# Roots for four latent heads at once, decay matrices by two wide products, and a first stage with its squares on VectorE and its rotary tables later

## The chip, the core and the metric

The kernel runs on one core of one Trainium2 chip. The core has five engines that run side by side, each through a list of its own: TensorE (PE in the profile; its weight loads are shown as PEld), VectorE (DVE), ScalarE (ACT), GpSimd (POOL) and SyncE (SP), which here issues the transfers between the chip's memory and the core's. The metric is device time in microseconds for one execution; smaller is better. The kernel before has a median of 1480.11 us over three runs (1479.24 to 1482.22).

## The reference

The program computes a four-part decoder trunk of two layers on x with 1024 tokens and 1024 channels, all in 32-bit floats. Cut to what the change touches:

```
def rmsnorm(x, g):
    xf = x.astype(jnp.float32)
    y = xf * lax.rsqrt(jnp.mean(xf * xf, axis=-1, keepdims=True) + EPS)
    return (y * g.astype(jnp.float32)).astype(x.dtype)
...
def even_layer(h, layer_idx, positions, w_in, ...):
    z = h @ w_in                       # h is rmsnorm(x)
    a_in, a_gate, q, k, v, b_gate = _split(z, EVEN_WIDTHS)
    ...
    q = partial_rope(rmsnorm(q, q_norm), positions, B_ROT, ROPE_THETA)
    k = partial_rope(rmsnorm(k, k_norm), positions, B_ROT, ROPE_THETA)
...
def odd_layer(h, positions, w_in, ...):
    q = (rmsnorm(cq, q_a_norm) @ w_uq).reshape(B, T, H_C, DQK_C)
    kv = (rmsnorm(ckv, kv_a_norm) @ w_ukv).reshape(B, T, H_C, D_NOPE + DV_C)
    ...
    q = rmsnorm(q, q_norm)             # 4 heads of 192, one root for each token and head
    k = rmsnorm(k, k_norm)
...
def gated_delta_rule(q, k, v, g, beta):
    gc = jnp.cumsum(g, axis=-1)
    gamma = jnp.exp(jnp.where(incl, gc[..., :, None] - gc[..., None, :], -jnp.inf))
```

Layer 0 holds a pooling mixer and differential attention, layer 1 latent attention (4 heads) and a gated DeltaNet (4 heads). Each layer ends in an output projection and a gated per-layer embedding.

## The kernel before

**Tiling.** Tokens are cut into blocks of 128 (eight of them, in two halves of 512), channels into chunks of 128 (eight). A large product is done with both operands split into a high and a low part in the F32R type, as three products of up to 512 columns (`mm3`, L142 to L144): high by high, high by low, low by high. The split is one ScalarE copy (L134, or L137 with a scale) and one VectorE subtract (L135, or L138). A product of plain F32 operands appears in the profile as two TensorE instructions. The eight accumulator banks of 512 columns have tags: acc (2), s (2), x (2), tr (1) and o (1).

**What sets the order.** Every engine runs its own list in order. The lists are laid out when the program is built, by a scheduler that goes by the order of the program and by estimated times, so that work later in the program can stand ahead of earlier work that is not ready by estimate: the profile shows a memset of L414 at 0.81 us, long before the loop of L356 begins.

**The first stage (0 to about 69 us).** The first loop (L356) goes over the eight chunks of x's first half. `load_x` (L322) loads a chunk, splits it (L137, L138) and squares it on ScalarE (L329, L332); from the second chunk on GpSimd adds the square to a running sum (L333). `wload` loads and splits the weights of the pool branch (L134, L135), and twelve products follow. After the second chunk the program has `rope_tables` (L193 to L230), which builds the cosine and sine of layer 0 from the positions: 56 VectorE instructions on tiles of at most 128x64, two Sin on ScalarE, four GpSimd writes. Their constants (the inverse frequencies) are loaded by a transfer of their own ahead of them, and another transfer after the loop (L369) loads the rest of the constants.

The second loop does the same for x's second half, with nine products a chunk. After its third chunk `finish_x(0)` turns the first half's sums into roots: eight small TensorE instructions (L182), ten small VectorE instructions (L121, L111 to L116, iterations of a root in integer and float steps), two copies, a VectorE product with the unit matrix (L187), a product with a matrix of ones (two TensorE instructions, L190) and a ScalarE copy (L191). The result is a row of roots that `pool_in` (L347, L350) needs to scale the accumulators. After the loop come `finish_x(1)`, one more group of 24 products, four more `pool_in`, the gain products of the tables (L407, GpSimd), and head 0 of the attention beside the pool branch `even_pool`, whose shifted adds run on GpSimd (L423).

**The latent q/k/v stage (about 758 to 850 us).** `mla_qkv` goes over eight token blocks and, in each, over two pairs of heads. A pair takes nine products into two banks: q of two heads (384 columns, six products) on tag s, k and v (512 columns, three products) on tag x. ScalarE squares the four head vectors and sums them (L808, L809), VectorE adds the shared rotary part (L810), finds the four roots (`mean_rsqrt`, L121 and L111 to L116: ten instructions in a chain) and scales the vectors (L814, L816); ScalarE copies v (L818), GpSimd does the rotation (L828 to L834), and a transfer takes the result out. Between the two pairs of a token block the program does one block of `gate_proj`: 24 products on an acc bank, a Tanh (L903) and a VectorE product (L904). `decay` (L843), placed ahead, computes the DeltaNet's log decays gd and, through bank o, three exponentials of sums of them (L870, L871).

**The DeltaNet preparation (about 868 to 1030 us).** `gdn_prep` runs eight times (four heads, two halves) beside the convolutions. For the decay matrix GpSimd multiplies the mask GT by the four columns of gd (L921), TensorE multiplies each of the four 128x128 results by the mask LE in F32 (L924, eight TensorE instructions), ScalarE takes the exponential (L925), and GpSimd cuts two triangles (L927). The tile of tag w4 (three buffers) holds the masked columns and the results.

Of the kernel before, what the change touches and what calls it, by code (L numbers as in the profile page):

```python
# [21 lines left out]
P = 128  # L22
# [34 lines left out]
def trunk_kernel(ctx, tc, a, out, layers=2):  # L57
# [26 lines left out]
    def bank(tag):  # L84
        return pp.tile([P, 512], F32, tag=tag, bufs=BANKS[tag], name=nm(tag))
# [236 lines left out]
    def load_x(h, k, sums):  # L322
# [5 lines left out]
        if k == 0:  # L328
            s.activation(sums, raw, AF.Square)  # L329
        else:  # L330
            sq = T("z", 2)
            s.activation(sq, raw, AF.Square)  # L332
            g.tensor_tensor(out=sums, in0=sums, in1=sq, op=ALU.add)  # L333
# [22 lines left out]
    for k in range(KC):  # L356
# [5 lines left out]
        if k == 1:  # L362
            dma.dma_start(cst[:, C_INVF:C_END], a["cst"][:, C_INVF:C_END])
            rtmp = T("g", 3, (3, 64))
            rtmp = [rtmp[:, i, :] for i in range(3)]
            cos0, sin0 = rope_tables(yp, 0, 8, lambda dt: rtmp.pop().bitcast(dt),
                                     lambda shape, dt, name: T("pt", 2, shape[1:], dt))
    second = [bank(n) for n in ("x", "x", "tr")]
    dma.dma_start(cst[:, P:C_INVF], a["cst"][:, P:C_INVF])  # L369
# [12 lines left out]
    for j in range(4):  # L382
        pool_in(second[j], j, 1)
    lvt = T("o", 2)[:, 0:256]
# [411 lines left out]
    def mla_qkv(we, h):  # L796


        for c in range(4):
            t = 4 * h + c  # L800
            for hp in range(2):
                wq, wk = we[hp]
                pq, pk = bank("s"), bank("x")
                proj_tok(la[0:2], wq, t, 384, pq)
                proj_tok(la[2:3], wk, t, 512, pk)
                ss, sq = S("qss", 4), T("sqj", 1, (192,))
                for j in range(2):
                    s.activation(sq, pq[:, 192 * j:192 * j + 192], AF.Square, accum_out=ss[:, j:j + 1])  # L808
                    s.activation(sq[:, 0:P], pk[:, P * j:P * j + P], AF.Square, accum_out=ss[:, 2 + j:3 + j])  # L809
                v.tensor_scalar(ss[:, 2:4], ss[:, 2:4], sskr[:, t:t + 1], None, ALU.add)  # L810
                r = mean_rsqrt(ss, 4, 192, "mla")
# [29 lines left out]
    qscale = gp.tile([P, H * NT], F32, name="qscale")  # L841

    def decay():  # L843
# [24 lines left out]
        for m, dst in ((LE, egc), (GT, egr), (ones, egl)):  # L868
            ps = bank("o")
            pe.matmul(ps[:, 0:32], m, gd.rearrange("p h t -> p (h t)"), start=True, stop=True)  # L870
            s.activation(dst, ps[:, 0:32], AF.Exp)  # L871

# [35 lines left out]
    def gdn_prep(hd, h, q, k, vT):  # L908
# [9 lines left out]

        gg = T("w4", 3, (T_,))
        gs, ge = gg[:, 0:512], gg[:, 512:1024]  # L920
        g.tensor_tensor(out=c3(gs), in0=GT.unsqueeze(1).to_broadcast([P, 4, P]), in1=bc(gd[:, hd, 4 * h:4 * h + 4]), op=ALU.mult)  # L921
        ps = bank("x")
        for c in range(4):
            pe.matmul(ps[:, c * P:(c + 1) * P], gs[:, c * P:(c + 1) * P], LE, start=True, stop=True)  # L924
# [404 lines left out]
```

## Time and profile before

| | |
|---|---|
| median of three runs | 1480.11 us (1479.24 to 1482.22) |
| the profiled execution: time, span | 1479.85 us, 1477.9 us |
| TensorE busy | 1419.0 us, 96% |
| VectorE busy | 985.1 us, 67% |
| ScalarE busy | 666.2 us, 45% |
| GpSimd busy | 207.0 us, 14% |
| TensorE's granted clock, mean | 0.991 |

The profile comes from one execution. A row of a group gives line, engine, operation, output and inputs, shapes and the count, then busy time with the mean of one in ns, then the idle time of the engine just before them and what ended it. A row of the timeline gives start and duration in us, and in brackets the idle time before it with the instruction that ended it. A row of the waits reads "engine, line waited for: us in total, times, longest". A row of stretches gives start, end and length in us, then the busy time and the instructions of PE, PEld, DVE, ACT and POOL, then the granted clock (1.00 is full), the share of the transfer engines and GB/s.

### The profile page before, as it was taken

To read this page: it belongs to the slowest core of one execution; us is meant where nothing else is said; L and a number is where in the kernel's file an instruction comes from. 1 tells how busy PE (TensorE), PEld (TensorE's weight loads), DVE (VectorE), ACT (ScalarE), POOL (GpSimd) and SP (SyncE) were. 2 spreads that over 40 slices of the span, in tenths; PEclk is the share of its full clock that TensorE was granted. 3 is DMA by queue.
4 is the path that set the end of the run, shared out by engine and by line. 5 is a ranking of instruction groups with operands and counts; after the bars stand their busy time and mean duration, and the time that the engine had idled before them with its cause. 6 is when DMAs were issued, how large, how long until landed. Compare 5 with 4: busy or idle time off the path is not lost.

```text
span 1477.9 us, 22765 instructions
## 1 busy us (share of the span) xinstructions
PE 1419.0 (96%) x7495; PEld 1158.4 (78%) x7495; DVE 985.1 (67%) x2918; ACT 666.2 (45%) x1660; POOL 207.0 (14%) x347
## 2 busy tenths in 40 slices
PE   7899999999999999999999999999989999999998
PEld 6678888888887778887777777888768888877886
DVE  8745667676676785356778888897557888643342
ACT  6325656565566733243554443434234455722220
POOL 4230101011111000022025511110000000000021
PEclk9999999999999999999999999999999999999999
DMA  5215323232333463333523432333576634343432
GB/s 188 83 47 139 84 75 93 65 108 51 100 94 100 147 211 107 108 122 115 111 64 153 170 122 97 116 128 122 183 250 199 206 124 143 119 149 100 128 107 86
DMA packets 127749, 181.52 MB, mean 123 GB/s; under 512 B 28536, under 2 KB 55440, under 8 KB 127632
## 3 DMA queue, kind: packets, MB, share of 16 engines
q1 hardware_dynamic: 127632, 180.08, 39.6%
q8 instruction: 59, 0.97, 0.3%
q14 instruction: 58, 0.48, 0.1%
HBM read 108.20 MB, written 52.95 MB: 109 GB/s over the span
## 4 chain that ended last, share of the span: by engine, by line
PE 70%; DVE 12%; ACT 7%; DMA 5%; issue 4%; POOL 1%; SPq 0%; DVEq 0%; ACTq 0%; POOLq 0%
PE acc L144 17%; PE acc L142 17%; PE acc L143 17%; PE o L268 4%; PE s L533 2%; PE tr L275 2%; DVE wl L135 1%; PE s L534 1%; DMA raw<-in_od_w_in 1%; ACT wh L134 1%; DVE p L257 1%; ACT sqj L917 1%; ACT p L261 1%; PE acc L1048 1%; DMA raw<-in_ev_w_in 1%
## 5 line engine op out<-in xcount | busy, mean ns | idle before, releaser
L142 PE MATMUL acc<-wh,x 128*128 128x512 f32 (+1 forms) x576 | 230.3, 400 | 0.9 <-DVE g L465 0.7
L143 PE MATMUL acc<-wl,x 128*128 128x512 f32 (+1 forms) x576 | 228.7, 397 | 1.9 <-DVE wl L135 1.9
L144 PE MATMUL acc<-wh,x 128*128 128x512 f32 (+1 forms) x576 | 227.1, 394 | 0.0
L144 PE MATMUL acc<-x,wl 128*128 128x512 f32 x504 | 201.9, 401 | 4.8 <-DVE wl L135 4.8
L142 PE MATMUL acc<-x,wh 128*128 128x512 f32 x504 | 203.6, 405 | 2.9 <-ACT wh L134 2.5
L143 PE MATMUL acc<-x,wh 128*128 128x512 f32 x504 | 200.7, 399 | 0.3 <-DVE x L138 0.3
L134 ACT CAST wh<-raw 128x512 fp32r<-128x512 f32 (+2 forms) x184 | 106.8, 600 | 87.4 <-PE acc L143 36.0
L135 DVE TENSOR_TENSOR wl<-raw,wh 128x512 fp32r<-128x512 f32 (+2 forms) x184 | 121.9, 681 | 28.2 <-ACT wh L134 26.1
L143 PEld LDWEIGHTS acc<-wl,x 128*128 128x128 f32 x576 | 108.5, 188 | 25.3 <-DVE wl L135 3.0
L142 PEld LDWEIGHTS acc<-wh,x 128*128 128x128 f32 x576 | 108.3, 188 | 24.0 <-PE acc L144 1.1
L144 PEld LDWEIGHTS acc<-wh,x 128*128 128x128 f32 x576 | 108.4, 188 | 22.3
L144 PEld LDWEIGHTS acc<-x,wl 128*128 128x128 f32 x504 | 95.6, 190 | 29.7 <-DVE wl L135 7.7
L142 PEld LDWEIGHTS acc<-x,wh 128*128 128x128 f32 x504 | 95.7, 190 | 26.1 <-ACT wh L134 3.5
L261 ACT ACTIVATE p<-p,mx 128x128 f32<-128x128 f32 (+7 forms) x128 | 99.4, 778 | 32.5 <-DVE mx L257 22.8
L143 PEld LDWEIGHTS acc<-x,wh 128*128 128x128 f32 x504 | 95.6, 190 | 22.2 <-DVE x L138 0.7
L676 POOL TENSOR_TENSOR u<-hp,hp 128x512 f32<-128x512 f32 x32 | 43.2, 1351 | 469.8 <-DMA out_T<-u 133.5
L143 PE MATMUL acc<-hp,wh 128*128 128x512 f32 x256 | 101.6, 397 | 0.0
L144 PE MATMUL acc<-hp,wl 128*128 128x512 f32 x256 | 101.5, 397 | 0.0
L142 PE MATMUL acc<-hp,wh 128*128 128x512 f32 x256 | 101.5, 396 | 0.0
L257 DVE CUSTOM_DVE_ANT_0 p<-s,cst 128x512 f32<-128x512 f32 (+3 forms) x128 | 74.2, 586 | 26.5 <-PE s L534 15.6
L674 DVE SCALAR_TENSOR_TENSOR th<-th,ld 128x512 f32<-128x512 f32 x32 | 26.9, 840 | 77.9 <-ACT th L672 76.0
L461 ACT ACTIVATE z<-acc,rstd 128x256 f32<-128x256 f32 x48 | 22.8, 474 | 102.4 <-PE acc L144 99.5
(487 smaller groups left out, 2902.3 us busy)
## 6 DMA issues: line engine op xcount, KB each, us to landing
raw<-in_ev_w_in SPq DMA_DIRECT2D x56, 256.0 KB
Q<-sq SPq DMA_DIRECT2D x96, 128.0 KB
qkv<-zz SPq DMA_DIRECT2D x16, 640.0 KB
raw<-cat SPq DMA_DIRECT2D x32, 256.0 KB
raw<-in_ple_w_gate SPq DMA_DIRECT2D x32, 256.0 KB
ld<-ple SPq DMA_DIRECT2D x32, 256.0 KB
zq<-qkv SPq DMA_DIRECT2D x16, 512.0 KB
K<-sq SPq DMA_DIRECT2D x48, 128.0 KB
```

The source lines that it names most:

```text
L134: s.copy(hi, src)
L135: v.tensor_tensor(out=lo, in0=src, in1=hi.bitcast(F32), op=ALU.subtract)
L142: pe.matmul(ps, lh, rh, start=first, stop=False)
L143: pe.matmul(ps, lh, rl, start=False, stop=False)
L144: pe.matmul(ps, ll, rh, start=False, stop=last)
L257: v.tensor_tensor_reduce(out=pm[:, c * 512:c * 512 + n], in0=ps[:, 0:n], in1=mk, scale=-scale, scalar=prev, op0=ALU.add, op1=ALU.min, accu ...
L261: s.activation(pm[:, 0:w], pm[:, 0:w], AF.Exp, bias=prev, scale=-1.0, accum_out=sums)
L268: pe.matmul(ps, pt[:, (blk % 4) * P:(blk % 4 + 1) * P], vals(blk), start=blk == 0, stop=blk == nblk - 1)
L275: pe.transpose(tr[:, b * P:(b + 1) * P], pm[:, (4 * c + b) * P:(4 * c + b + 1) * P], ident)
L533: pe.matmul(ps[:, 0:n], q[:, m, qs], k[:, m, 0:n], start=True, stop=False)
L674: v.scalar_tensor_tensor(out=th, in0=th, scalar=1.0, in1=r, op0=ALU.add, op1=ALU.mult)
L676: g.tensor_tensor(out=u, in0=hi.bitcast(F32), in1=lo.bitcast(F32), op=ALU.add)
```

## The change

It has three parts. In the first stage, `load_x` adds the squares on VectorE instead of GpSimd; the two transfers of constants become one, after the first loop; and `rope_tables` moves from the second chunk of the first loop to behind the eighth `pool_in`. In `mla_qkv`, both pairs of a token block are projected and squared first, one call finds all eight roots, and then both pairs are scaled; the banks go round over three pairs, (s, x), (s, x) and (tr, o), so that the head pair number 2t + hp takes bank pair (2t + hp) % 3. The generator still yields after each scaled pair, so the program now issues both projections, the roots and the first pair's scaling, then the gate block, then the second pair's scaling. For the decay matrices, gd is split once into two F32R parts, GT is copied once into F32R, GpSimd multiplies LE by the four columns of each part, and TensorE accumulates two products of 512 columns with GT as weights; the masked columns have a w4 tile of their own.

```
-            g.tensor_tensor(out=sums, in0=sums, in1=sq, op=ALU.add)
+            v.tensor_tensor(out=sums, in0=sums, in1=sq, op=ALU.add)
...
-        if k == 1:
-            dma.dma_start(cst[:, C_INVF:C_END], a["cst"][:, C_INVF:C_END])
-            rtmp = T("g", 3, (3, 64))
-            rtmp = [rtmp[:, i, :] for i in range(3)]
-            cos0, sin0 = rope_tables(yp, 0, 8, lambda dt: rtmp.pop().bitcast(dt),
-                                     lambda shape, dt, name: T("pt", 2, shape[1:], dt))
     second = [bank(n) for n in ("x", "x", "tr")]
-    dma.dma_start(cst[:, P:C_INVF], a["cst"][:, P:C_INVF])
+    dma.dma_start(cst[:, P:C_END], a["cst"][:, P:C_END])
...
     for j in range(4):
         pool_in(second[j], j, 1)
+    rtmp = T("g", 3, (3, 64))
+    rtmp = [rtmp[:, i, :] for i in range(3)]
+    cos0, sin0 = rope_tables(yp, 0, 8, lambda dt: rtmp.pop().bitcast(dt),
+                             lambda shape, dt, name: T("pt", 2, shape[1:], dt))
...
         for c in range(4):
             t = 4 * h + c
+            ss, sq, pqk = S("qss", 8), T("sqj", 1, (192,)), []
             for hp in range(2):
                 wq, wk = we[hp]
-                pq, pk = bank("s"), bank("x")
+                pq, pk = [bank(n) for n in (("s", "x"), ("s", "x"), ("tr", "o"))[(2 * t + hp) % 3]]
+                pqk.append((pq, pk))
                 proj_tok(la[0:2], wq, t, 384, pq)
                 proj_tok(la[2:3], wk, t, 512, pk)
-                ss, sq = S("qss", 4), T("sqj", 1, (192,))
                 for j in range(2):
-                    s.activation(sq, pq[:, 192 * j:192 * j + 192], AF.Square, accum_out=ss[:, j:j + 1])
-                    s.activation(sq[:, 0:P], pk[:, P * j:P * j + P], AF.Square, accum_out=ss[:, 2 + j:3 + j])
-                v.tensor_scalar(ss[:, 2:4], ss[:, 2:4], sskr[:, t:t + 1], None, ALU.add)
-                r = mean_rsqrt(ss, 4, 192, "mla")
+                    n = 4 * hp + j
+                    s.activation(sq, pq[:, 192 * j:192 * j + 192], AF.Square, accum_out=ss[:, n:n + 1])
+                    s.activation(sq[:, 0:P], pk[:, P * j:P * j + P], AF.Square, accum_out=ss[:, n + 2:n + 3])
+                v.tensor_scalar(ss[:, 4 * hp + 2:4 * hp + 4], ss[:, 4 * hp + 2:4 * hp + 4], sskr[:, t:t + 1], None, ALU.add)
+            rr = mean_rsqrt(ss, 8, 192, "mla")
+            for hp in range(2):
+                (pq, pk), r = pqk[hp], rr[:, 4 * hp:4 * hp + 4]
                 zz = T("zz", 2, (2, 640))
...
+    gdp = [gp.tile([P, H, NT], F32R, name=n) for n in ("gdh", "gdl")]
+    GTr = ip.tile([P, P], F32R, name="GTr")
+    s.copy(GTr, GT)
...
+        split(*gdp, gd)
...
+        gg, ps = T("w4", 3, (T_,), F32R), bank("x")
+        for i, part in enumerate(gdp):
+            gi = gg[:, 512 * i:512 * i + 512]
+            g.tensor_tensor(out=c3(gi), in0=LE.unsqueeze(1).to_broadcast([P, 4, P]),
+                            in1=bc(part[:, hd, 4 * h:4 * h + 4].bitcast(F32)), op=ALU.mult)
+            pe.matmul(ps, GTr, gi, start=i == 0, stop=i == 1)
         gg = T("w4", 3, (T_,))
         gs, ge = gg[:, 0:512], gg[:, 512:1024]
-        g.tensor_tensor(out=c3(gs), in0=GT.unsqueeze(1).to_broadcast([P, 4, P]), in1=bc(gd[:, hd, 4 * h:4 * h + 4]), op=ALU.mult)
-        ps = bank("x")
-        for c in range(4):
-            pe.matmul(ps[:, c * P:(c + 1) * P], gs[:, c * P:(c + 1) * P], LE, start=True, stop=True)
         s.activation(ge, ps, AF.Exp)
```

## The prediction

> **What bounds the kernel now.** I read the page first, then the table of stretches around the three edits, then TensorE's waits there, and last the timeline.
>
> ```profile
> span 1477.9 us, 22765 instructions
> PE 1419.0 (96%) x7495; PEld 1158.4 (78%) x7495; DVE 985.1 (67%) x2918; ACT 666.2 (45%) x1660; POOL 207.0 (14%) x347
> PE   7899999999999999999999999999989999999998
> ```
>
> TensorE is busy 96% of the span; nothing else comes near. A change pays only if it removes TensorE work or a moment in which TensorE stands still. About 59 us of standing still is all there is.
>
> ```profile
> core 0: us, PE busy (x) PEld busy (x) DVE busy (x) ACT busy (x) POOL busy (x), PEclk, DMA share, GB/s
> 6.50:34.74 28.24, 26.65 (x97) 20.75 (x98) 26.35 (x50) 18.60 (x33) 15.16 (x11) 0.94 0.63 206
> 34.74:62.56 27.82, 21.68 (x92) 16.76 (x90) 19.37 (x58) 8.50 (x14) 9.07 (x17) 0.88 0.16 54
> 62.56:69.33 6.77, 6.76 (x28) 4.90 (x28) 5.37 (x19) 3.81 (x7) 0.00 (x0) 1.00 0.49 144
> 69.33:90.00 20.67, 19.98 (x83) 15.20 (x82) 12.71 (x21) 8.16 (x17) 12.78 (x11) 1.00 0.23 68
> 756.00:792.00 36.00, 32.87 (x150) 25.55 (x148) 33.24 (x139) 18.27 (x72) 15.11 (x30) 1.00 0.41 134
> 792.00:843.00 51.00, 46.37 (x211) 38.31 (x211) 39.41 (x152) 23.74 (x100) 26.08 (x62) 1.00 0.43 163
> 868.00:1030.00 162.00, 159.03 (x817) 130.84 (x816) 143.11 (x345) 71.16 (x212) 21.30 (x32) 1.00 0.34 111
> ```
>
> The rows are the first loop over x, the second loop, the last group of products before head 0, head 0's first products beside the pool branch, the latent q/k/v stage (two rows), and the DeltaNet preparation. The loops lose 1.6 and 6.1 us and run below full clock; the latent stage loses 3.1 and 4.6; the last row is dense, so there only less TensorE work pays.
>
> **Part 1: squares on VectorE, tables later.** What slows the first loop is in the timeline:
>
> ```profile
> 14.24 4.95 POOL L333 TENSOR_TENSOR o<-o,z 128x512 f32<-128x512 f32 x3 [0.28 <-ACT z L332]
> 14.84 1.26 DVE L206 TENSOR_SCALAR g<-g 128x64 int32<-128x64 int32 x1
> 16.75 0.50 PE L144 MATMUL acc<-x,wl 128*128 128x512 f32 x1 [1.28 <-DVE wl L135]
> 18.11 0.63 PE L143 MATMUL s<-x,wh 128*128 128x512 f32 x1
> 20.67 0.63 PE L143 MATMUL acc<-x,wh 128*128 128x512 f32 x1
> 26.56 0.18 DVE L206 TENSOR_SCALAR g<-g 128x64 int32<-128x64 int32 x1
> 34.04 0.40 PE L142 MATMUL s<-x,wh 128*128 128x512 f32 x1
> 34.27 0.40 PE L143 MATMUL s<-x,wh 128*128 128x512 f32 x1
> 41.03 0.95 PE L182 MATMUL o<-cst,o 128*128 128x1 f32 x8
> 41.84 0.48 PE L142 MATMUL x<-x,wh 128*128 128x512 f32 x1
> 44.50 0.40 PE L144 MATMUL x<-x,wl 128*128 128x512 f32 x1
> 45.60 0.26 ACT L224 ACTIVATE g<-g 128x64 f32<-128x64 f32 x1 [6.76 <-DVE g L223]
> 47.79 0.15 DVE L121 TENSOR_SCALAR tokm<-o 128x4 f32<-128x4 f32 x1
> 50.19 0.69 DVE L187 TENSOR_TENSOR sq<-cst,rstd 128x512 f32<-128x512 f32 x1
> 51.03 2.04 PE L190 MATMUL o<-sq,cst 128*128 128x512 f32 x2 [6.14 <-DVE sq L187]
> ```
>
> The same 128x64 instruction takes 0.18 us alone and 1.26 us beside GpSimd's add: VectorE waits out GpSimd's instruction. The Trainium skill ("SBUF — State Buffer", section "SBUF: two separate sides") calls this an exclusive lock on a port pair, held for the whole instruction; the two rows agree.
>
> ```profile
> line engine op names shapes xcount | busy us, mean ns | idle before us <-releasers
> L217 DVE TENSOR_TENSOR pt<-pt,pt 128x64 f32<-128x64 f32 x11 | 5.8, 524 | 0.2
> L213 DVE SCALAR_TENSOR_TENSOR pt<-g 128x64 f32<-128x64 f32 x12 | 4.8, 398 | 0.0
> L135 DVE TENSOR_TENSOR wl<-raw,wh 128x512 fp32r<-128x512 f32 x7 | 4.8, 679 | 0.0
> ```
> ```profile
> L333 POOL TENSOR_TENSOR o<-o,z 128x512 f32<-128x512 f32 x14 | 20.5, 1467 | 25.8 <-ACT z L332 25.3
> L423 POOL TENSOR_TENSOR p<-p 128x1039 f32<-128x1039 f32 (+4 forms) x5 | 10.6, 2118 | 15.1 <-DVE p L347 12.4 <-DVE p L435 2.5
> ```
>
> *Removed and added.* Fourteen GpSimd adds (20.5 us) go; 14 VectorE adds come, priced by the subtract of equal shape (679 ns): 9.5 us. The table code issues 56 small VectorE instructions (8 on L203, 12 each on L212 and L213, 11 on L217, 13 others). The two table rows above average 0.4 and 0.5 us where a free one takes about 0.2 (26.56); without GpSimd beside them all 56 cost some 11 us.
>
> *First loop.* VectorE needs 0.75 + 0.68 + 0.68, about 2.1 us a chunk (the 0.75 is estimated from the equal-sized rows plus a scalar operand), TensorE 12 products at 0.233 us (34.04 to 34.27), 2.8 us. So VectorE stays ahead, and the tables cannot stand in the way: their frequencies are now loaded behind the first loop. What goes is the 1.6 us of waits and the slow clock behind them (from 18.11 to 20.67 six products, 0.43 us apart instead of 0.233; with their two neighbours eight times 0.2, 1.6 us). I add 0.3 for the earlier transfer no longer in the queue: 3.5 us. The Trainium skill ("TensorE: Matmul & The Clock Gate", section "What's actually happening") says the clock falls only after an idle window of about 3.4 us; the 0.63 us product stands behind a 1.28 us wait, and the measurement decides. By the page those slow products are not the wait's doing, the gain would be 1.6 us smaller and the time 1462.6.
>
> *Second loop.* L121, the head of the roots that L190 needs, ran at 47.79, 6 us after its input, since the whole table chain lay ahead of it on VectorE. Now the tables come later in the program than finish_x(0) and the pool inputs, and can only fill gaps. The chain takes 3.1 us (47.79 to 50.88); the 12 products from 41.84 to 44.73 cover 2.9, so 0.2 to 0.7 stays. The stretch becomes 72 products at 0.233 (16.8), twice 0.8 for L182, 1.0 for L190 (2.04 at half clock) and 0.4 left over: 19.8 instead of 27.8, 8.0 gained. What is late next is nothing on TensorE: the last products (third row) are dense already.
>
> *Where the tables go.* About 11 us of VectorE work fills 22 to 51 us, where x's second half (16 instructions, about 11 us) and the pool inputs leave room. Their two Sins now come behind the pool gates' Tanh, at worst one ScalarE table load more in a stretch where ScalarE is busy 8.5 of 27.8 us: nothing, as long as VectorE is on time; before, ScalarE stood 6.76 us at L224 with head 0's casts queued behind it, and that wait shrinks with VectorE's backlog. GpSimd's four table writes and eight gain products stand ahead of the shift-adds, as they did; nothing that TensorE needs soon comes from there. On SP the constants' second transfer joins the third: one issue less. Part 1: -11.5 us; bounds -12.2 (no wait left), -3.5 (the tables still ahead of L121) and +2 (the third rival).
>
> **Part 2: roots for four heads at once.**
>
> ```profile
> PE s L142 <- DVE zz L814: 4.9, 6, 1.1
> PE acc L144 <- DVE wl L135: 2.1, 2, 1.5
> ```
> ```profile
> L814 DVE SCALAR_TENSOR_TENSOR zz<-s,mlay,gq 128x192 f32<-128x192 f32 x20 | 8.2, 412 | 1.3 <-DVE mlay L116 1.1
> L808 ACT ACTIVATE sqj<-s 128x192 f32<-128x192 f32 x20 | 6.6, 332 | 0.5
> L115 DVE SCALAR_TENSOR_TENSOR newton<-newton 128x4 f32<-128x4 f32 x18 | 5.0, 276 | 0.6
> ```
>
> Between 756 and 870 us TensorE waited six times for L814 to free a bank. One root chain per row block instead of two takes ten instructions of about 0.25 us off VectorE, 2.5 us of each 10; eight columns cost what four did. The new wait: both pairs are held until the common chain is through. Behind the second pair's last product come four squares (0.33 us each and, by estimate, 0.1 between: 1.7 us), the chain (2.5) and the first pair's four scalings (1.3): some 5.5 us. Covering it are a gate block (24 products, 5.6) and the next block's first pair on the third pair of banks (six of 384 columns and three of 512, 1.75): 7.3. On ScalarE the two copies L818 wait for the scalings with the gate's Tanh L903 queued behind; L903 frees an acc bank that is wanted one gate block later, so nobody waits for that. So the six waits go: -4.9 us. I give nothing for the 2.1 us of weight waits. Bounds: -7.7, all the loss in both rows of the stage, and +22 (the last rival).
>
> **Part 3: decay matrices.**
>
> ```profile
> 874.91 1.13 PE L924 MATMUL x<-cst,w 128*128 128x128 f32 x8 [0.98 <-ACT sqj L917]
> 875.79 0.48 PE L144 MATMUL acc<-x,wl 128*128 128x512 f32 x1
> ```
> ```profile
> L921 POOL TENSOR_TENSOR w<-cst,gd x8: 1032/1040/2287, 844.0 to 976.0; 128x512 f32<-128x512 f32 x8
> ```
>
> Eight TensorE instructions (each F32 product is two) take 0.88 us, eight times. Two products of 512 columns in F32R take 0.47: 0.41 saved, 3.3 us in all, on a TensorE that is busy 159 of 162. GpSimd's 8 masks become 16 at 1.04 us; it is busy 21 of 162, so the cost is only what VectorE waits beside them: at most 8.3 us on an engine with 19 free. I take 0.7. The split of gd and the copy of GT are three instructions of about 0.2 us beside other work. Part 3: -2.6, bounds -4.3 and +1.
>
> **Sum.** -11.5 - 4.9 - 2.6 = -19.0. The profiled execution took 1479.85 us (its span and 1.95 around it), 0.26 below the median of the three runs. From the median: 1461.0 us.
>
> **Rivals.**
> *The tables still come first (0.14).* If VectorE's list again has them ahead of L121, only the first loop gains: 1461 + 8 = 1469. For it: up to L121 VectorE has no less to do than before, 9.5 us of adds for some 12 us of waiting. Against: the tables are later in the program.
> *The latent wait returns (0.12).* Bank o is single and serves decay's three products too; if a pair waits for it or for tr in every block, part 2 gives nothing: 1466. Against: those three come once.
> *The tables beside the shift-adds (0.06).* L423 holds GpSimd five times for 2.1 us while head 0 starts (fourth row of the stretches). If the tables are put there, two-input table instructions wait out all of it, 10.6 us; with the 11 us of their own VectorE has 21.6 us more in a stretch of 20.7 where 8 are free. Head 0's banks are released up to 13.6 us late: 1475 at worst. This is what the lock named above would do. Against: gaps come earlier.
> *Slower: the gate blocks run out (0.08).* If the pair on tr and o waits long, the gate blocks run ahead, and the last of the eight row blocks have no products to cover the 5.5 us behind them. Part 2 then loses its 4.9 and 5.5 for each bare block: three give 1482, no change; from the fourth on (1488) the kernel is slower. For it: TensorE's order is fixed beforehand, by estimates. Against: TensorE lost only 4.6 us in the 51 of the sixth row, so gates and pairs have alternated to the end so far.
>
> **The numbers.** My forecast has 0.60, from 1456 to 1466. The first three rivals lie within 1475 and the bounds of parts 1 to 3 that are still likely reach down to 1455; outside are the last rival and a tail of the first, less than 2 in 10. A measurement here can tell about 0.2% (3 us) from no change. Faster: 0.92, the forecast and three rivals; the same: 0.03, three bare blocks; slower: 0.05, more of them.
>
> **What would show it.** Right: head 0's first product at 57 to 58.5 us instead of 69.33; no TensorE wait before L190 above 1 us; small table instructions all near 0.2 us; no waits for L814 in the latent stage; two F32R products per decay matrix. Wrong: L121 long after L182 in VectorE's list; TensorE waiting in the latent stage for L814 or bank o; rows of L814 with no gate product beside them.

## The result and the profile after

The changed kernel takes 1471.15 us (median of five runs, 1467.55 to 1473.87) against 1480.19 us before on the same chip (five runs): the ratio is 0.9943, with a 95% interval of 0.9931 to 0.9954. That is 9.0 us, less than half of the 19.0 that the sum gave. The profiled execution took 1472.82 us. Its page and its table of stretches, cut at the same events as before (first loop, second loop, the products ahead of head 0, head 0's beginning in two rows, the DeltaNet preparation):

```profile
span 1471.1 us, 22586 instructions
PE 1415.7 (96%) x7447; PEld 1153.8 (78%) x7447; DVE 977.9 (66%) x2853; ACT 664.6 (45%) x1662; POOL 195.9 (13%) x341
```
```profile
core 0: us, PE busy (x) PEld busy (x) DVE busy (x) ACT busy (x) POOL busy (x), PEclk, DMA share, GB/s
6.50:30.50 24.00, 23.71 (x95) 19.08 (x96) 21.94 (x35) 20.74 (x37) 0.10 (x1) 1.00 0.73 250
30.50:50.20 19.70, 19.54 (x90) 15.42 (x88) 9.79 (x31) 3.20 (x6) 0.00 (x0) 1.00 0.23 73
50.20:57.00 6.80, 6.79 (x29) 5.00 (x30) 5.41 (x20) 3.64 (x7) 0.00 (x0) 1.00 0.41 126
57.00:70.00 13.00, 9.85 (x39) 7.51 (x39) 12.22 (x25) 4.91 (x10) 8.28 (x6) 0.93 0.26 78
70.00:90.00 20.00, 19.43 (x74) 14.09 (x73) 16.79 (x56) 8.03 (x16) 8.29 (x18) 0.96 0.12 39
868.00:1000.00 132.00, 124.99 (x612) 100.25 (x611) 120.67 (x282) 54.47 (x162) 24.99 (x34) 1.00 0.35 115
```

Both loops are dense and at full clock, and the second takes 19.7 us where 19.8 was forecast. Then comes what was not forecast: from 57 to 70 us TensorE is busy 9.85 of 13 us while VectorE is busy 12.22 of 13, and in the DeltaNet preparation TensorE, before busy 159 of 162, now stands still 7 of 132.

To see where time comes and goes, I count TensorE's products: the first product of every three is line 142 in all these kernels, so the start of the n-th of them can be compared between two traces, each counted from its own first. The numbers are us earlier (-) or later (+) than in the kernel before; each kernel has one profiled execution, and the runs are explained below.

```
n      us before  changed     p1  p1sums     p2     p3      t0  t0_smask
48         56.15   -12.36  -12.39  -10.11  -2.28  -1.44  -12.04   -11.75
96         95.67    -7.16   -7.36  -10.56  -2.66  -1.84  -12.27   -11.96
768       734.02    -3.08   -9.97   -9.79  -2.22  -0.15  -14.23   -11.61
912       843.21    -7.75   -9.93   -9.74  -6.87  -0.16  -19.04   -16.20
960       885.94   -11.67  -10.39   -9.92  -8.08  -0.25  -23.02   -20.81
1104     1014.18    -7.43  -10.51   -9.99  -7.75  +2.41  -18.75   -23.62
1440     1461.21    -6.97   -9.29   -7.87  -4.52  +2.84  -16.99   -22.57
```

In the changed kernel 12.4 us are gained by 56 us of the kernel before, late in the second loop, and 12.3 are still there at head 0's first product (69.33 before); 5.2 go back by 96 us, 4.7 are gained in the latent stage (734 to 843), 3.9 right behind it, and 4.2 go back in the DeltaNet preparation (886 to 1014). Between 96 and 734 us nothing is changed, yet this execution loses 4.1 there; the 16 kernels run later have between -2.6 and +1.7 on the same code, and the five executions of the changed kernel differ by 6.3 us among themselves, so a loss of this size in one execution is not put down to the edit (more on it at the end). The kernel before had such a loss too, in its first loop: p2 and p3, whose first stage is that of before, are 1.4 to 2.3 us earlier by 56 us.

The waits of TensorE in the changed kernel, from three windows (55 to 110, 745 to 842, 868 to 1010 us; the columns are us in total, times, longest):

```profile
PE acc L143 <- DVE wl L135: 3.2, 1, 3.2
...
PE s L142 <- DVE zz L816: 1.0, 1, 1.0
...
PE tr L142 <- DVE zz L816: 0.5, 1, 0.5
...
PE x L921 <- DVE sp L966: 2.7, 2, 1.5
PE acc L144 <- DVE wl L135: 2.0, 4, 0.8
PE acc L142 <- ACT wh L134: 1.6, 1, 1.6
```

The first is new. The next two come from the eight heads' scalings, where there were six waits for L814 (4.9 us). Of the last three, the waits for L966 and for the cast L134 are new. The timeline shows what surrounds the first:

```profile
38.04 0.16 DVE L121 TENSOR_SCALAR tokm<-o 128x4 f32<-128x4 f32 x1 [4.51 <-PE o L182]
...
50.67 0.16 DVE L121 TENSOR_SCALAR tokm<-o 128x4 f32<-128x4 f32 x1 [3.12 <-PE o L182]
...
56.82 0.76 DVE L203 TENSOR_SCALAR g<-cst,npos 128x8 f32<-128x8 f32 x5
...
62.01 3.89 DVE L352 SCALAR_TENSOR_TENSOR Q<-z,Q 128x512 f32<-128x512 f32 x2 [0.76 <-ACT z L351]
...
65.92 0.68 DVE L135 TENSOR_TENSOR wl<-raw,wh 128x512 fp32r<-128x512 f32 x1
66.66 0.50 PE L143 MATMUL acc<-wl,x 128*128 128x512 f32 x1 [3.15 <-DVE wl L135]
...
71.01 1.84 DVE L213 SCALAR_TENSOR_TENSOR pt<-g 128x64 f32<-128x64 f32 x1
72.89 2.42 DVE L217 TENSOR_TENSOR pt<-pt,pt 128x64 f32<-128x64 f32 x1
...
75.44 0.23 DVE L213 SCALAR_TENSOR_TENSOR pt<-g 128x64 f32<-128x64 f32 x1
...
70.86 4.37 POOL L421 TENSOR_TENSOR p<-p 128x1036 f32<-128x1036 f32 x2
```

VectorE stood still for 4.51 and 3.12 us ahead of the two roots, but its list has the first table instruction only behind the second root, at 56.82. So the tables met the shift-adds (L421): the same L213 takes 1.84 us beside one and 0.23 us when it is over, at 75.44.

The wait of 3.15 us, however, ends at 66.66, before those instructions, and no wait of TensorE names them. It is for a weight split, L135, that stands in VectorE's list behind L352, whose two instructions take 3.89 us beside the shift-adds. In the kernel before, the same split stood ahead of L352:

```profile
72.28 0.84 DVE L135 TENSOR_TENSOR wl<-raw,wh 128x512 fp32r<-128x512 f32 x1
...
75.02 3.02 DVE L352 SCALAR_TENSOR_TENSOR Q<-z,Q 128x512 f32<-128x512 f32 x2
```

L352 was held up there too (3.02 us), but TensorE had its split by then. So the tables cost by the order that the list got with them in it, more than by the time that they waited out themselves. Of the 5.2 us given back, 3.15 are this wait and about 1.6 the slow products behind it (from 68.22 to 71.20 they start 0.43 us apart; the granted clock is 0.66 from 66.6 to 71.6).

### The profile page after: what moved, and what is told of

It is laid out like the page before. It is cut to its first block, busy times and chain, and to the rows that moved or that the text cites. A ratio compares the mean times of both kernels' runs of the same rounds, so it can differ in the third digit from the quotient of the medians.

```text
span 1471.1 us, 22586 instructions
## 1 busy us (share of the span) xinstructions
PE 1415.7 (96%) x7447; PEld 1153.8 (78%) x7447; DVE 977.9 (66%) x2853; ACT 664.6 (45%) x1662; POOL 195.9 (13%) x341
## 5 line engine op out<-in xcount | busy, mean ns | idle before, releaser
L135 DVE TENSOR_TENSOR wl<-raw,wh 128x512 fp32r<-128x512 f32 (+2 forms) x184 | 124.5, 698 | 31.8 <-ACT wh L134 30.2
L134 ACT CAST wh<-raw 128x512 fp32r<-128x512 f32 (+2 forms) x184 | 105.9, 600 | 69.4 <-PE acc L143 22.6
L672 DVE SCALAR_TENSOR_TENSOR th<-th,ld 128x512 f32<-128x512 f32 x32 | 30.0, 937 | 75.7 <-ACT th L670 75.7
```

Of the source, the lines that this page charges most:

```text
L134: s.copy(hi, src)
L135: v.tensor_tensor(out=lo, in0=src, in1=hi.bitcast(F32), op=ALU.subtract)
L672: v.scalar_tensor_tensor(out=th, in0=th, scalar=1.0, in1=r, op0=ALU.add, op1=ALU.mult)
```

## The experiments

My theory after the result: the mechanisms of the forecast hold, but the tables landed beside the shift-adds, and the doubled masks cost more than the narrow products did. The rivals: head 0 is bounded there by its weights or the pool branch whatever the tables do, and the loss in the DeltaNet preparation is one of order or phase, not of the masks.

**Each part alone.** Runs p1, p2 and p3 are the kernel before with one part of the change each; the diffs are those of the change.

p1: 

> The kernel before with part 1 alone: squares on VectorE, constants joined, tables after the pool inputs. Theory: the loops gain 12.4 us by head 0's first product, and about 5.6 of it go back between 75 and 96 us, where the tables lie beside the shift-adds: 6 to 7.5 us faster than before, about 1473. Rival (nothing given back for the tables' sake; the loss at 75 to 96 came from the other parts): 11.5 to 12.5 faster, about 1468.

p2: 

> The kernel before with part 2 alone: one root for four heads, third pair of banks. Theory: the six waits of the latent stage go, 4.9 us, and perhaps the 2.1 us of weight waits and the slow clock behind them at 843 to 878: 5 to 8 us faster, 1472 to 1475. Rival (the latent stage's gain came only with the other start of the kernel): within 2 us of before.

p3: 

> The kernel before with part 3 alone: decay matrices by two wide products. Theory: GpSimd's second mask and the second tile of the ring of three cost TensorE more than the 3.3 us of narrow products: 1 to 5 us slower than before, and the stretch from 868 to 1000 us longer by that. Rival (the part is worth what was forecast and the loss in the changed kernel came from another phase of the weights): 2.6 us faster, about 1477.5.

Measured: p1 1472.34 us, ratio 0.9970 (0.9958 to 0.9981); p2 1473.38 us, 0.9972 (0.9962 to 0.9982); p3 1482.06 us, 1.0028 (1.0017 to 1.0038). By the table, p1 gains 12.4 us and gives back 5.0 us between 56 and 96 us with no other part present, p2 gains 4.65 us between 734 and 843, and p3 loses 2.7 between 886 and 1014. The theory's place is right for all three, but p1's time moved by 5.0 us and p2's by 4.0, less than the 6 to 7.5 and 5 to 8 expected (p2 loses 3.2 us behind 1014 us); for p1 the first loops of p2 and p3 may say why. They have none of part 1, yet their first loop is 3.4 to 3.7 us shorter by 29 us, with no slow clock, and all of that but 1.4 to 2.3 us goes into a longer wait for L187. In p2's timeline:

```profile
49.23 2.05 PE L190 MATMUL o<-sq,cst 128*128 128x512 f32 x2 [6.90 <-DVE sq L187]
```

VectorE's chain sets the time of this product, whatever the first loop takes. So part 1's first stage is worth 12.4 us against the profiled execution of before and 10.1 to 10.9 against these two. The third part alone makes the kernel slower, by 0.3%. p1 and p1tab have the split L135 behind L352 as the changed kernel has it.

**The tables: where they may stand.** tabmid, t0 and s23 are the changed kernel with the tables elsewhere. In tabmid they follow `finish_x(0)`:

```
         if k == 2:
             finish_x(0, sums[0])
+            rtmp = T("g", 3, (3, 64))
+            ...
+            cos0, sin0 = rope_tables(...)
...
-    rtmp = ...; cos0, sin0 = rope_tables(...)     # behind the eighth pool_in
```

> The changed kernel with the rotary tables' code moved up, to stand right behind the first half's root in the second loop, so that VectorE's list has them among the pool inputs of the first half. Theory: they fill the standstills of VectorE between 41 and 57 us, little of them is left for the shift-adds, and 3 to 5.6 us come back: 1466 to 1468. Rival (what bounds head 0 after the loops is not the tables but its weights or the pool branch itself): within 1.5 us of the changed kernel. Second rival (in the loop they delay the roots again): slower than the changed kernel.

Measured: 1469.38 us, ratio 0.9945 (0.9932 to 0.9958), no better than the change. The rival's number came, but not for its reason, as the timeline of tabmid shows:

```profile
61.70 1.49 DVE L217 TENSOR_TENSOR pt<-pt,pt 128x64 f32<-128x64 f32 x1
63.11 0.68 DVE L350 TENSOR_TENSOR Q<-tr,g 128x512 f32<-128x512 f32 x1
63.71 1.68 DVE L220 TENSOR_SCALAR g<-pt 128x64 f32<-128x64 f32 x2
65.31 0.68 DVE L350 TENSOR_TENSOR Q<-acc,g 128x512 f32<-128x512 f32 x1
...
66.04 0.80 PE L142 MATMUL acc<-wh,x 128*128 128x512 f32 x1 [2.59 <-DVE Q L350]
```

The tables now stand among the instructions of the second half's root, and their tail among its pool inputs, again beside shift-adds. L350, which frees an acc bank, comes late, and TensorE waits 2.59 us for it: another wait than in the changed kernel, again for something in VectorE's list that stands among held-up instructions.

t0 moves them to the first chunk of the second loop:

```
     for k in range(KC):
         load_x(1, k, sums[1])
+        if k == 0:
+            rtmp = T("g", 3, (3, 64))
+            ...
+            cos0, sin0 = rope_tables(...)
```

> The changed kernel with the rotary tables' code moved up once more, to the first chunk of the second loop, so that VectorE's list has one table instruction between every two of x's second half (24 to 42 us) and none beside the second half's root, the pool inputs or the shift-adds. Theory: what is given back between 56 and 96 us comes from VectorE being full there, of table instructions that wait out shift-adds above all; with the tables gone from it, at least 3 of the 5.2 us come back and the first half's root is at most 2 us later: 2 to 5 us faster than the changed kernel, ratio to before about 0.991 to 0.993. Rival (head 0 is bounded there by the pool branch or by weights, whatever the tables do): the wait reappears on another line between 60 and 80 us, ratio 0.994.

Measured: 1464.07 us, ratio 0.9900 (0.9885 to 0.9914). In the timeline of t0 one or two table instructions stand between every two of x's, all at their free duration, and the table of stretches has the place that was lost:

```profile
26.46 0.21 DVE L213 SCALAR_TENSOR_TENSOR pt<-g 128x64 f32<-128x64 f32 x1
26.60 0.68 DVE L333 TENSOR_TENSOR o<-o,z 128x512 f32<-128x512 f32 x1
```
```profile
57.00:70.00 13.00, 13.00 (x55) 10.00 (x54) 9.07 (x14) 5.00 (x10) 8.75 (x9) 1.00 0.32 98
```

TensorE is busy 13.00 of 13 us instead of 9.85. Of the 5.2 us given back nothing is left (-12.04 at 56 us, -12.27 at 96); the first half's L187 is at 42.01 instead of 40.23, and TensorE is 0.3 us later for it by 56 us. In t0's list the split L135 (60.14) stands ahead of L352 (62.88) again. So it is shown that the place of the tables costs the 5.2 us; the weights and the pool branch, unchanged, bound nothing. That table instructions which wait out shift-adds do it, as the expectation has it, is true of tabmid and not of the changed kernel.

s23 puts the tables and transfers back where they were in the kernel before and keeps the squares on VectorE and parts 2 and 3. p1sums is the kernel before with the squares alone on VectorE, p1tab with the table edit alone, the sums still on GpSimd.

s23: 

> The changed kernel with the tables and the constants' transfers back where they were; squares on VectorE, parts 2 and 3 kept. Theory (the moved tables only cost): TensorE's wait for L187 is about 1.2 us, nothing is given back from 56 to 96 us, 10.5 us gained by then instead of 7.2: 3 us faster than the changed kernel, ratio 0.992. Rival (the later tables pay elsewhere): the changed kernel's 0.994 or more.

p1sums: 

> The kernel before with the squares' sums on VectorE alone; tables and constants where they were. Theory (the sums' half of part 1 is the first loop's): the first loop gains 3.5 to 4.3 us, TensorE's wait for L187 stays 4 to 6 us since the table chain is ahead of it on VectorE; nothing is given back at 75 us: 4 us faster, ratio 0.997. Rival (the table chain was slow only by GpSimd's adds): it is through before the first half's root, both loops gain, 8 to 12 us, ratio 0.992 to 0.994.

p1tab: 

> The kernel before with the tables later and the constants joined, sums still on GpSimd. Theory: without tables ahead of it the first half's root is on time, so most of the second loop's 6 to 8 us are gained, the first loop gains only what the tables took from VectorE, and 5 go back beside the shift-adds: about 2 to 4 us faster than before, ratio 0.997 to 0.999. Rival: GpSimd's adds end late and the root with them, no faster than before.

Measured: s23 1466.95 us, ratio 0.9921 (0.9908 to 0.9934), as expected, with a wait for L187 of 1.2 us and nothing given back from 56 to 96 us; p1sums 1469.62 us, 0.9951 (0.9935 to 0.9967); p1tab 1474.03 us, 0.9962 (0.9950 to 0.9975), a little better than expected. In p1sums the rival won (8.0 us by the medians, the ratio a little above its range), and a term of my prediction falls with it: the table chain had been as late as that only because of GpSimd's adds. Its group of L217 and its wait for L187:

```profile
L217 DVE TENSOR_TENSOR pt<-pt,pt 128x64 f32<-128x64 f32 x11 | 2.4, 221 | 0.0
...
PE o L190 <- DVE sq L187: 1.2, 1, 1.2
```

524 ns a piece before, 221 ns now; the wait of 6.1 us is 1.2. Either edit alone brings most of the gain by 56 us (the sums 10.1, the tables 11.7 of 12.4); with the sums moved, the later tables add 2.3 us there and then cost 5.

**Part 3: masks, ring, or order.** p12 is the changed kernel without part 3; t0_12 is t0 without it; onemask forms one mask and one product, so the low part of gd is left out; zzmask takes the masks' tile from another ring:

```
-        gg, ps = T("w4", 3, (T_,), F32R), bank("x")
+        gg, ps = T("zz", 2, (2, 640), F32R), bank("x")
```

p12: 

> The changed kernel without part 3 (decay matrices as before). Theory: part 3 by itself costs 3 to 4 us, so this is 3 to 4 us faster than the changed kernel, ratio to before 0.991 to 0.992, and the stretch from 868 to 1010 us has no wait for the weights' cast of 1.6 us. Rival (parts do not add): the same as the changed kernel, ratio 0.994.

onemask: 

> The changed kernel with only the high part of gd in the decay matrices: one mask and one wide product, the low part left out. Second tile of the ring of three kept. Theory (the doubled masks beside VectorE's weight splits cost most of part 3's loss): about 2.5 to 4 us faster than the changed kernel, of which 1.9 are the eight products left out (8 times 0.233). Rival (the second tile of the ring, or the changed order of ScalarE's casts, costs it whatever the number of masks): not more than 2 us faster.

zzmask: 

> The changed kernel with the masks in the ring of the latent stage's output rows, which is free by then, so that no mask waits for the previous matrix's last reader. Theory (the wait for the ring puts the masks beside the weight splits): masks early, no wait of L921 for L966, 2 to 4 us faster than the changed kernel. Rival (the masks' work itself, or the order of the casts): within 1 us of the changed kernel.

t0_12: 

> Parts 1 and 2 with the tables at the first chunk of the second loop, decay matrices as before. Theory (the gains of the two repairs add): 12.0 from part 1, 8 to 9 from part 2, none from part 3, so 18 to 21 us faster than before less what the clock takes: ratio 0.986 to 0.989, about 1460. Rival (the start's gain is lost again at the heads' weights in the DeltaNet preparation): 0.990 or more.

Measured: p12 1466.38 us, ratio 0.9914 (0.9900 to 0.9928), as expected; onemask 1463.94 us, 0.9900 (0.9884 to 0.9915), 6 us faster than the changed kernel by the ratios, more than expected, but 3.3 us faster by counted products from 886 to 1014 us, of which 1.4 are the products left out there; that leaves 1.9 for the second mask. zzmask 1469.13 us, 0.9935 (0.9922 to 0.9947), about 1 us faster by the ratios, which speaks for the rival: the ring was not it. t0_12 came out at 1462.86 us, 0.9907 (0.9891 to 0.9924), and missed what was expected; its ratio is the rival's, but not the rival's place. It has no loss in the preparation, but of the 3.9 us that most kernels with part 3 gain between 843 and 886 us it gains 0.8 (p12 2.7). Why is open, below.

nomask and dmask take the two halves of part 3 apart. nomask has the wide products and no mask at all, so its decay matrices are not computed; dmask has both masks and the narrow F32 products:

```
 nomask:
-            g.tensor_tensor(out=c3(gi), in0=LE..., in1=bc(part...), op=ALU.mult)
-            pe.matmul(ps, GTr, gi, start=i == 0, stop=i == 1)
+            pe.matmul(ps, GTr, hn1[i][h][0], start=i == 0, stop=i == 1)
...
 dmask:
+        for i in range(2):
+            gi = gg[:, 512 * i:512 * i + 512]
+            g.tensor_tensor(out=c3(gi), in0=GT..., in1=bc(gd...), op=ALU.mult)
+            for c in (2 * i, 2 * i + 1):
+                pe.matmul(ps[:, c * P:(c + 1) * P], gi[:, c * P:(c + 1) * P], LE, start=True, stop=True)
```

nomask: 

> The changed kernel without any mask on GpSimd: the two wide products per decay matrix read tiles of the activations, as wide and of the same type, and the exponential is scaled by 0.001; the decay matrices are not computed. Theory A (GpSimd's masks beside VectorE's weight splits make the loss): nothing is lost from 886 to 1010 us, and this is 3 to 4 us faster than onemask's place, 5 to 7 faster than the changed kernel. Theory B (the loss is the place of the last head's weight cast behind a Tanh in ScalarE's list, which the shorter products moved): the waits for the cast of 1.6 us stay, and it is within 3 us of the changed kernel.

dmask: 

> The changed kernel with its two masks and its second tile, but the narrow F32 products of before, two from each mask. Theory A (masks): 870 to 1010 us as slow as in the changed kernel or 3 us slower, ratio 0.994 to 0.997. Theory B (order of ScalarE's list, moved by the wide products): no wait for the cast of 1.6 us, the time that of the changed kernel without part 3 plus what VectorE waits beside the second masks, ratio 0.9915 to 0.993.

Measured: nomask 1460.47 us, ratio 0.9893 (0.9875 to 0.9910); dmask 1471.66 us, 0.9962 (0.9948 to 0.9976). By counted products, from 886 to 1014 us nomask gains 3.5 us, dmask loses 6.6, the changed kernel loses 4.2 and p12 0.2. dmask's time is what theory A gave, though TensorE waits for no cast there. The forecast for the wide products is 2.5 us in this stretch (six matrices), and nomask's 3.5, which has no mask at all, fits it. With and without GpSimd's masks the changed kernel and nomask lie 7.7 us apart: that is what both masks of a matrix cost here, one of which the kernel before has too. How much of it is the second mask alone is less clear. Between p12 and dmask, with the same narrow products, lie 6.4 us, but dmask's masks also have their own tile and stand at another place in GpSimd's list; onemask gives 1.9. Each figure is from one execution. How the masks cost time is in the changed kernel's timeline, at the third head's start:

```profile
924.10 0.63 ACT L895 ACTIVATE gz<-cv 128x512 f32<-128x512 f32 x1 [2.72 <-DVE cv L893]
924.63 0.49 ACT L134 CAST wh<-raw 128x384 fp32r<-128x384 f32 x1
...
924.93 1.42 POOL L928 TENSOR_TENSOR w<-cst,gdh 128x512 fp32r<-128x512 f32 x1 [0.71 <-DVE sp L966]
...
925.37 3.18 DVE L135 TENSOR_TENSOR wl<-raw,wh 128x384 fp32r<-128x384 f32 x3
...
925.18 0.50 PE L142 MATMUL acc<-x,wh 128*128 128x512 f32 x1 [1.58 <-ACT wh L134]
...
926.82 0.73 PE L144 MATMUL acc<-x,wl 128*128 128x512 f32 x2 [0.47 <-DVE wl L135]
```

Three weight splits take 3.18 us beside the masks, 1.06 each, instead of the 0.55 of a free one. And a weight cast stands behind a Tanh (L895) that waits 2.72 us for VectorE, so TensorE waits 1.58 us for the cast. nomask has the same Tanh with the same 2.72 us, and the cast behind it, but TensorE does not wait there: in the changed kernel VectorE is 1.58 us further behind TensorE. Where it falls behind is one head earlier, in the chain of the roots (L113, L114). First the kernel before, then the changed kernel:

```profile
912.74 1.04 POOL L921 TENSOR_TENSOR w<-cst,gd 128x512 f32<-128x512 f32 x1 [13.51 <-DVE sp L958]
...
918.28 0.10 POOL L879 MEMSET z<- 128x3 f32 x1 [4.50 <-DVE gm L929]
918.48 0.17 DVE L113 TENSOR_TENSOR newton<-gdny 128x8 f32<-128x8 f32 x1
918.68 0.17 DVE L114 SCALAR_TENSOR_TENSOR newton<-newton,gm 128x8 f32<-128x8 f32 x1
```
```profile
908.43 0.10 POOL L885 MEMSET z<- 128x3 f32 x1 [20.46 <-DVE gm L937]
908.50 1.04 POOL L928 TENSOR_TENSOR w<-cst,gdh 128x512 fp32r<-128x512 f32 x1
908.63 0.93 DVE L113 TENSOR_TENSOR newton<-gdny 128x8 f32<-128x8 f32 x1
...
909.59 0.97 DVE L114 SCALAR_TENSOR_TENSOR newton<-newton,gm 128x8 f32<-128x8 f32 x1
```

Before, the mask ran 5.5 us ahead of a memset that waits for VectorE. Now the masks stand behind that memset in GpSimd's list, wait 20.46 us with it, and start together with the root chain, whose two instructions take 0.93 and 0.97 us instead of 0.17 each: 1.56 us, as much as the wait. So the rival of order holds in part: what seems to cost here is the masks' place in GpSimd's list, though no run moved it alone. zzmask has the same place, so the masks' ring is not what moved them; what did was not tried. The largest new wait, 2.7 us for L966, ends both times before GpSimd's masks there begin (880.48 and 968.88 against 880.89 and 968.97), so these masks do not cause it; whether VectorE's lateness does was not tried.

The waits for the splits (wl) are the smaller part, some 2 of the 7 us that TensorE stands still between 886 and 1014. The group of these splits from 868 to 1010 us, in the kernel before (one mask a matrix), in the changed kernel (two) and in nomask (none):

```profile
L135 DVE TENSOR_TENSOR wl<-raw,wh 128x384 fp32r<-128x384 f32 x23 | 14.2, 633 | 0.4 <-ACT wh L134 0.4
```
```profile
L135 DVE TENSOR_TENSOR wl<-raw,wh 128x384 fp32r<-128x384 f32 x23 | 17.0, 770 | 0.0
```
```profile
L135 DVE TENSOR_TENSOR wl<-raw,wh 128x384 fp32r<-128x384 f32 x21 | 11.0, 549 | 1.4 <-ACT wh L134 1.4
```

**Is it GpSimd's hold on VectorE, or the work?** Both masks go to another engine, in t0:

```
 t0_vmask:
-            g.tensor_tensor(out=c3(gi), in0=LE.unsqueeze(1)...
+            v.tensor_tensor(out=c3(gi), in0=LE.unsqueeze(1)...
 t0_smask:
+            for c in range(4):
+                s.activation(gi[:, c * P:(c + 1) * P], LE, AF.Identity, scale=part[:, hd, 4 * h + c:4 * h + c + 1].bitcast(F32))
```

t0_vmask: 

> The kernel with the tables at the first chunk of the second loop (run t0), both masks of the decay matrices on VectorE, 0.69 us each. Theory (the loss is GpSimd's hold on VectorE, 2.8 us for a pair of masks that VectorE's splits wait out): 1.4 us of VectorE's own time cost less than 2.8 of waiting; the 3.6 us that t0 loses from 886 to 1010 shrink to 1 or less: 2 to 4 us faster than t0, ratio 0.987 to 0.989. Rival (VectorE is simply full there, and any work of that size on it costs the same): no faster than t0, ratio 0.990 or more.

t0_smask: 

> The same with both masks on ScalarE, as eight scaled copies of 128 columns, 0.28 us each. Theory (the hold on VectorE is the loss): VectorE is free of it, but 2.2 us more on ScalarE stand ahead of weight casts: between t0 and 3 us faster. Rival (ScalarE's casts decide at a head's change): slower than t0 by 2 us or more, with longer waits for the cast.

Measured: t0_vmask 1460.15 us, ratio 0.9870 (0.9857 to 0.9882); t0_smask 1457.31 us, 0.9850 (0.9838 to 0.9863). From 886 to 1014 us t0 loses 4.3 us, t0_vmask 1.7, and t0_smask gains 2.8. t0_vmask keeps more of the loss than the 1 us expected, t0_smask is better than expected. The masks on VectorE itself cost less than on GpSimd, so GpSimd's hold is the larger cost, though VectorE's own time counts too; off both, nothing is lost, and t0_smask's 7.1 us against t0 agree with the 7.7 of nomask. The masks' own group and the weight splits of t0_smask:

```profile
L930 ACT ACTIVATE w<-cst,gdl 128x128 fp32r<-128x128 f32 x24 | 7.8, 389 | 0.0
...
L135 DVE TENSOR_TENSOR wl<-raw,wh 128x384 fp32r<-128x384 f32 x19 | 10.1, 551 | 2.2 <-ACT wh L134 2.2
```

ScalarE takes 0.39 us for each of eight pieces, more than the 0.28 expected, and is busy 683.6 us of the span instead of 664.6; TensorE does not wait for it more than 0.3 us. t0_smask beats both kernels: 21.5 us faster than the one before.

One profile does not fit: s23, part 3 unchanged, loses 8.4 us from 886 to 1014 us, twice what the changed kernel loses. Some 3.4 of it are slow products (the granted clock is 0.91 from 867 to 904 us). The others with two masks on GpSimd lose between 2.7 (p3) and 6.6 (dmask), so a figure of a few us for this stretch from one execution is rough.

## Why the prediction was wrong, point by point

- **First stage to head 0.** Right in its sum: forecast -11.5, came -12.4, -4.3 by 29 us (forecast -3.5) and -8.1 in the second loop (-8.0). The wait before L190 fell from 6.1 to 0.2 us, and head 0's first product starts at about 57 us instead of 69.33. But the first loop's term was no gain of the edit: p2 and p3 have it without the edit, and that the number came was luck. Against them the stage is worth 10.1 to 10.9 us, most of it because VectorE's chain is no longer late (the wait before L190 is 6.7 us shorter than in p2).
- **"Where the tables go."** This step failed. It said that 11 us of VectorE work "fills 22 to 51 us", because VectorE has room there. It has, but the list, laid out beforehand, did not use it: the tables came at 56.82 to 86 us, beside the shift-adds. With them there, the list has the weight split L135 behind L352, which the shift-adds hold, and 5.2 us go back. The place is that of the third rival, which had 0.06; its mechanism is mostly another, since it had table instructions wait out all of the shift-adds and release banks up to 13.6 us late, where TensorE waited 3.15 us for a split. A place in the program's order is not a place in time: t0 and tabmid, the same code some lines apart, have ratios of 0.9900 and 0.9945 and lie 4.5 us apart by 96 us.
- **The first half's root was late "since the whole table chain lay ahead of it".** True of the trace, but the chain was long mostly because of GpSimd's adds (524 ns against 221). The two edits were summed as if each had its own gain; p1sums shows that the first alone brings 10.1 of the 12.4 us. The first rival (1469) fails with it: it took tables ahead of L121 to cost the second loop's 8 us, and without GpSimd's adds they cost 2.3 us by 56 us, 1.2 of it the wait for L187.
- **Part 2.** Right: forecast -4.9, came -4.7 in the changed kernel and -4.65 alone. The six waits went, but the forecast had no wait left, and 1.5 us of waits for L816 stand in their place. TensorE's standing still from 734 to 843 us fell from 8.8 to 5.1 us, by 3.7; where the other 1.0 us comes from was not found, so part of the agreement is luck. The slower rival did not come: gate products covered the chain to the last block.
- **Part 3.** This step failed in its second term. The products were right (0.41 us a matrix forecast; in p3 the products behind a matrix start 0.41 to 0.45 us earlier). For the masks I took 0.7 us of the bound of 8.3, since VectorE had 19 us free. From 886 to 1014 alone both masks cost 7.7 us (nomask against the changed kernel), the second one between 1.9 (onemask) and 6.4 us (dmask, which has more changed). The free time was an average over 162 us; what counts is where a mask meets an instruction that TensorE's next work depends on: the root chain, held from 0.17 to 0.93 and 0.97 us, and the splits at a head's start. Nor did the bound of +1 follow from the terms: -3.3 and 8.3 make +5.0, and the +4.2 measured lies within that.
- **Nothing given for the weight waits** behind the latent stage: the changed kernel gained 3.9 us between 843 and 886, p2 alone 1.2, t0_12 0.8. The waits there (2.1 us before) and the slow clock after them come and go from kernel to kernel. What decides it was not found. It may be a part of why the three parts alone, -5.0, -4.0 and +4.7 us by medians with intervals of some 1.6 us to either side, do not add up to -9.0; the rest stays open.

## What to carry to other kernels

A step that is moved in the program goes where the list, not the idle time, has room: name the instructions that it will stand beside and those that it pushes back, and look for a GpSimd instruction beside them. Price extra GpSimd work not by the free time of GpSimd or VectorE but by the VectorE instruction that must wait it out at the moment when TensorE's next work depends on it, and look at what GpSimd's list has ahead of it: here a memset that waited sent two masks off beside the root chain. And when two edits remove the same obstacle, undo each alone before both are kept: here the one that was needed least carried the cost.

## What the runs showed of the hardware

**GpSimd holds VectorE up where the two meet.** The mean of a 128x384 split from 868 to 1010 us was 549, 633 and 770 ns with none, one and two GpSimd masks a matrix (nomask, before, changed), but 552 ns in zzmask, which has two masks at other moments. Two 128x8 instructions rose from 0.17 to 0.93 and 0.97 us beside masks of 1.04 us, and a 128x64 table instruction rose from 0.23 to between 1.84 and 2.42 us beside shift-adds of 1.9 to 2.4 us. The Trainium skill ("SBUF — State Buffer", section "SBUF: two separate sides") describes an exclusive lock held for a whole instruction; the traces agree. Instructions with one input wait too: a copy (L215) takes 1.98 us at 68.85 in the changed kernel and 0.18 us in t0, and two of L220 take 1.68 us in tabmid.

**The clock after the same wait differs from trace to trace.** Every one of these kernels has, near 470 us, the same wait of 1.71 us for GpSimd's last step of a rotation (L242). In 16 of the 18 traces, one of each kernel, the clock stayed full behind it; in two it fell, in the changed kernel's and in zzmask's. What decides it is not known. The stretch around the wait, in the changed kernel and in t0:

```profile
468.70:475.50 6.80, 5.09 (x30) 4.69 (x29) 2.63 (x12) 2.96 (x11) 1.82 (x5) 0.75 0.11 40
```
```profile
463.70:470.50 6.80, 5.09 (x39) 4.56 (x38) 4.18 (x17) 4.58 (x16) 1.81 (x5) 1.00 0.11 40
```

The same busy time holds 30 instructions in the one and 39 in the other: 1.6 us of the changed kernel's loss between 96 and 734 us. The Trainium skill ("TensorE: Matmul & The Clock Gate", section "What's actually happening") says that the gate looks at a window of about 3.4 us that runs freely and does not reset when a kernel starts. No run here shows the window; that the same wait is followed by slow products in some traces and not in others fits it, but a wait of half that length came before them here. The slow products behind the wait of 1.28 us in the first loop of before, which I counted as gained, were in that execution and not in p2 or p3. But these have no wait above 0.33 us there, so whether the wait made the products slow stays open.
